# Weight casts to DRAM started one by one on semaphores of attention exponentials, and a scheduler with three new costs

## The chip, the cores and the metric

One Trainium2 chip; the program runs on all 8 cores, each with one sequence of the batch. The metric is device time in microseconds (us) of the slowest core. In a slow execution the cores of one die show a lower granted clock and the time is longer. A ratio compares the fast runs of two kernels of the same rounds on the same chip; it is not quite the ratio of the quoted medians. "Before" differs between chips, so experiments are compared by their ratios to it, given with a 95% interval.

## The reference, cut to what matters

One decoder layer: 2048 tokens and 16 learned meta tokens, width 1024. Two causal attentions with 8 heads each work on the same normalised input; their outputs are gated, added and projected; then a gated MLP with a short convolution follows.

```python
def hybrid_mixer(h, w_in, ...):
    proj = h @ w_in
    o_mla  = causal_block_attention(q_mla, k_mla, v_mla, MLA_QK_DIM ** -0.5)      # first attention
    o_fox  = causal_block_attention(fq, fk, fv, FOX_HEAD_DIM ** -0.5, cum)        # second attention
    gates  = sigmoid(gate_logit + b_gate)
    merged = g_mla * (o_mla @ w_branch_mla) + g_fox * (o_fox @ w_branch_fox)      # the merge
    return merged @ w_out                                                        # w_o
def conv_glu_ffn(h, w_up, conv_w, conv_b, w_down):                               # w_u, w_dn
    up = h @ w_up
    gate, val = up[..., :D_FF], up[..., D_FF:]
    return (silu(causal_depthwise_conv(gate, conv_w, conv_b)) * val) @ w_down
```

## The kernel before

The weights of merge (w_c), output projection (w_o) and MLP (w_u, w_dn) come in float32. The kernel has them cast by DMAs that GpSimd issues: w_c and w_u from DRAM to the bfloat16 scratches scr_c and scr_u, which are loaded tile by tile later, w_o and w_dn straight into SBUF. The casts of w_c, w_u and w_o, 68 transfers, are meant to run beside the two attentions.

The program doesn't write instructions in their final order. It records them with their dependencies, and a list scheduler with a clock of its own (cost tables for instructions, one serial bus for transfers) chooses each engine's order. Then the order is replayed, and semaphore waits are derived from data dependencies.

```python
def dma(self, eng, out, in_, prio=None, key=None, after=None):      # recorder
    ...
    self._dep(it, [in_], [out])
    if after is not None:
        it.preds.add(after)          # only the scheduler knows of it
# replay:
    if it.dma is not None:
        S.dma(e, it.key, kw["out"], kw["in_"])       # no wait for "after" comes out of this
```

So "after" was a hint. GpSimd was stopped by the order of its own stream and by the transfer that used the same one of eight keys before (idle up to 21.4 us at a time for a cast to scr_u, core 4). The casts were recorded in groups behind each pair of heads:

```python
def cast(n, after):
    ...
    for _ in range(n):
        if casts:
            K.dma("pool", *casts.pop(0), key="pc", after=after)
...
    done = heads_out(g, omT[:, p, c0:c0 + n], ot)
    cast(1 if s < 6 else 2, done)            # first attention, 20 steps
...
    done = heads_out(g, of[:, p, 0:n], ot)   # second attention
    if g == 0 and p < 4:                     # two w_o casts a step in the first group of rows
        ...
    else:                                    # later, three scr_u casts a step
        cast(3, done)
```

The load queue (SyncE) is in order as well: scr_c and scr_u tiles, rows of x, and stores of merge results (scr_h) go through it one behind the other (core 4: a store goes out at 465.87 us, for 0.33 us, and the scr_c load recorded behind it at 466.28).

The softmax here doesn't subtract the row's maximum and nothing guards it: scores larger than these inputs give would overflow.

Of the kernel before, what the change touches and what calls it, by code (L numbers as in the profile page):

```python
# [26 lines left out]
class Sched:  # L27
# [71 lines left out]

    def _add(self, eng, fn, reads, writes, dma_key=None):  # L100
        dma = dma_key is not None
# [4 lines left out]
        else:  # L106
            lst = self.cstream[eng]
            stream = eng
            op = _Op(eng, stream, len(lst) + 1, fn, False)
        deps = set()  # L110
        if dma and lst:
            deps.add(lst[-1])
# [71 lines left out]

    def dma(self, eng, key, out, in_, **kw):
        return self._add(eng, lambda e: e.dma_start(out=out, in_=in_, **kw), [in_], [out], dma_key=key)  # L186

# [134 lines left out]
class Item:  # L322
    __slots__ = ("idx", "alts", "tiles", "preds", "succ", "left", "ready", "dma", "bytes", "done", "start", "end", "eng", "prio", "key")

class Recorder:
    RES = {"pe": 165.0, "act": 100.0, "dve": 72.0, "pool": 45.0, "sp": 0.0}
    SEM = {"pe": 145.0, "act": 98.0, "dve": 107.0, "pool": 144.0, "sp": 120.0}
    SLACK = 10.0
    RATE = 250.0
    LAND = {"sp": 2000.0, "pool": 2300.0}  # L330
# [42 lines left out]
    def _item(self, alts, prio):  # L373
        it = Item()
        it.idx = len(self.items)
        it.alts = alts
        it.tiles = []
        it.preds = set()
        it.succ = []
        it.dma = None  # L380
        it.bytes = 0
        it.done = False
        it.ready = 0.0
        it.end = 0.0
        it.eng = None
        it.prio = prio
        it.key = None
        self.items.append(it)
        return it
# [53 lines left out]
    def cost(self, eng, name, args, kw):  # L443
        if name == "row pair":
            return max(self.cost(eng, "matmul", (), k) for k in args) + 12.0
        o = args[0] if name == "memset" else kw["out"]
# [18 lines left out]
        b16 = all(self._n(v)[1].dtype == BF16 for v in ins) and ap.dtype == BF16  # L465
        rate = 1.0
        if name == "reciprocal":
            rate = 8.0
        elif name in ("tensor_copy", "tensor_scalar", "memset"):
            rate = (0.5 if (not ps or b16) else 1.0)  # L470
            if b16 and not ps:
                rate = 0.25
        elif name == "tensor_tensor" and b16:
            rate = 0.5
        if name == "bn_stats":
            n = self._n(kw["in_"])[0]
        return n * rate * 1.042 + (125.0 if name == "scalar_tensor_tensor" and n > 8 else 66.0)

# [21 lines left out]
    def any(self, alts, prio=None):  # L500
        e0, name, args, kw = alts[0]
        wr = []
        rd = []
        for q in (args if name == "row pair" else (kw,)):
            wr += [q[k] for k in ("out", "accum_out") if isinstance(q.get(k), (View, bass.AP))]
            rd += [v for k, v in q.items() if k not in ("out", "accum_out") and isinstance(v, (View, bass.AP))]
        if name == "memset":
            wr = [args[0]]
        al = []
        for (e, nm, ar, k) in alts:  # L510
            al.append((e, nm, ar, k, self.cost(e, nm, ar, k)))
        it = self._item(al, {e: self._prio(e, prio) for (e, _, _, _) in alts})
        self._dep(it, rd, wr)
        return it
# [14 lines left out]
    def dma(self, eng, out, in_, prio=None, key=None, after=None):  # L529
# [6 lines left out]
        if after is not None:  # L536
            it.preds.add(after)
        return it

    def order(self):  # L540
# [12 lines left out]
        ev = []  # L553
        keyend = {}
        bus = [0.0]
        out = []
# [81 lines left out]
        while ev:  # L638
# [51 lines left out]
            if it.dma is not None:  # L690
# [9 lines left out]
                finish(it, "sp", st, end)  # L700
            else:
                freet[e] = st + dur
                out.append((it, alt))
# [18 lines left out]
    def replay(self):  # L722
        S = self.S

        def res(v):
            return v.at(v.t.slot) if isinstance(v, View) else v

        for it, (e, name, args, kw, _d) in self.done:
            if name == "row pair":
                for q in args:  # L730
                    S.op(e, "matmul", **{k: res(v) for k, v in q.items()})
                continue
            kw = {k: res(v) for k, v in kw.items()}
            if it.dma is not None:
                S.dma(e, it.key, kw["out"], kw["in_"])
            else:
                S.op(e, name, *[res(a) for a in args], **kw)

# [11 lines left out]
GT = ((0, 1, 2, 3), (4, 5, 6), (7, 8, 9), (10, 11, 12), (13, 14, 15, 16))  # L750
MID = (2, 5, 8, 11, 15)
FG = ((16, 384), (400, 384), (784, 384), (1168, 384), (1552, 512))
O_QLAT, O_KVLAT, O_KROPE, O_FQ, O_FK, O_FV, O_FLOG, O_GATE = 0, 384, 512, 544, 1056, 1568, 2080, 2088
# [10 lines left out]
def build_program():  # L764
# [28 lines left out]
    with contextlib.ExitStack() as es:  # L793
# [310 lines left out]
        ATT = {"pe": 2, "act": 3, "": 2}  # L1104

        def head(g, h, lhs, q, V, scale, bias, ot):
            c0, n = gcols(g)
# [4 lines left out]
            for kt in range(ts[-1] + 1):  # L1112
# [4 lines left out]
                kw = {} if bias is None else {"bias": bias(kt)}  # L1117
                K.op("act", "activation", out=pt[:, a:n], in_=ps[:, a:n], func=AF.Exp, scale=scale, **kw)
                if kt >= ts[0]:
# [52 lines left out]

        casts = [(scr_c[c, :, a:a + 1536], d_c[c, :, a:a + 1536]) for c in range(8) for a in (0, 1536)]
        casts += [(scr_u[j, :, a:a + 1024], d_u[j, :, a:a + 1024]) for j in range(NJ) for a in (0, 1024)]

        def cast(n, after):
            K.base = {"": 1.5}
            for _ in range(n):
                if casts:
                    K.dma("pool", *casts.pop(0), key="pc", after=after)  # L1180

        for s, (p, g) in enumerate([(p, g) for g in range(5) for p in (0, 1)] + [(p, g) for p in (2, 3) for g in range(5)]):
# [7 lines left out]
            for b in range(2):  # L1190
                h = 2 * p + b
                kt_ = KT[(p % 2) * 2 + b]
                head(g, h, lambda kt: kt_[:, kt * 128:kt * 128 + 128], qs[b], Vm, 96.0 ** -0.5, None, ot)
            done = heads_out(g, omT[:, p, c0:c0 + n], ot)
            cast(1 if s < 6 else 2, done)
            if s == 9:
# [20 lines left out]
        for i in range(4):  # L1217
            q_ = at(207488 + i * 1024, 512)
            K.op("pool", "memset", q_[64:128, :] if i < 2 else q_[0:64, :], 0.0, prio=2.5)
        QA = ring("qa", 207488, 512, 2)  # L1220
        QB = ring("qb", 209536, 512, 2)
# [9 lines left out]
        def attn_fox(g):  # L1231
# [8 lines left out]
            for p in range(4):  # L1240
# [10 lines left out]
                for b in range(2):  # L1251
                    h = 2 * p + b
                    head(g, h, lambda kt: Kf[:, p, kt * 128:kt * 128 + 128], qs[b], Vf, 0.125, lambda kt: bi[:, kt * 8 + h:kt * 8 + h + 1], ot)
                done = heads_out(g, of[:, p, 0:n], ot)
                if g == 0 and p < 4:
                    K.base = {"": 2.5}
                    for k in (2 * p, 2 * p + 1):
                        K.dma("pool", wo[:, k, :], d_o[:, k * 1024:k * 1024 + 1024], after=done)
                else:
                    cast(3, done)  # L1260
            return of
# [41 lines left out]
        for g in range(5):  # L1303
# [4 lines left out]
            merge(g, ofs[g])  # L1308
        K.close(OF, WC, SG, MG, H16, XS)

        K.base = {"": 6}
# [131 lines left out]
```

## Time and profile before

| | before |
|---|---|
| median of 6 runs | 1183.71 us (1180.92 to 1188.01) |
| spans of the 8 cores, profiled run | 1170.8 to 1181.1 us |
| TensorE busy, slowest core | 1107.8 us of 1181.1 |
| waits of TensorE with no named releaser, slowest core | 8.0 us |

A core's span is the time from its first to its last instruction. In the lines of the profile PE is TensorE, PEld its weight loads, DVE VectorE, ACT ScalarE, POOL GpSimd and SP SyncE; a q behind a name is the engine's sequencer. "Issue" is time in which an engine waited for nothing that the profile names. "Busy" TensorE does not mean TensorE at its peak: from 155 to 236 us on core 3 the row shows it busy for 79.3 of 81 us, but the matmuls started there are only 73.8 us of work (the measure is explained under "Where the time came from"). They are strung out behind the exponentials, with ScalarE busy for 75.2 us.

The profile follows the work back from the last instruction, at each step to what released it. This is a part of that chain, on core 4, around 466 us (start, length, what; all in us):

```profile
462.71 3.10 DVE SB L183 x4
...
465.87 0.33 SPq L186
...
466.28 15.20 DMA SB<-scr_c
...
481.62 5.08 PE PS L183 x40
```

A store of a merge result had to wait for VectorE (462.71); the scr_c load stood behind it in the load queue; and the load then took 15.2 us, while the median of all such loads is 5.4 us. TensorE waited only 0.6 us for it; it went on with attention, busy for 14.0 of the 16 us from 466 to 482 us, with ScalarE busy for 12.8.

### The profile page before, as it was taken

Reading aid. Unit: us, or ns where it says so; the run is one execution under the profiler, and the core shown is the slowest. Engines: PE = TensorE matmul, PEld = TensorE weight load, DVE = VectorE, ACT = ScalarE, POOL = GpSimd, SP = SyncE. Lnnn points to the kernel's source line nnn. Section 1 sums busy time; section 2 is a strip of 40 time slices with the busy share of each in tenths; the row PEclk is TensorE's granted clock in tenths of the full one; section 3 lists DMA queues with packets and bytes.
Section 4 is the critical chain, followed back from the end, with each engine's and each line's share of the span. In section 5 each row is a group of like instructions: output and inputs, shape, how many; then the busy total and the mean of one; then the engine's idle time right before and its main releaser. Section 6 shows DMA issues by size and latency. Waiting matters only on the chain.

```text
span 1181.1 us, 25481 instructions; the slowest of 8 cores (1170.8 to 1181.1 us)
## 1 busy us (share of the span) xinstructions
PE 1107.8 (94%) x8345; PEld 621.5 (53%) x8345; DVE 777.8 (66%) x1737; ACT 637.8 (54%) x1383; POOL 104.3 (9%) x187
## 2 busy tenths in 40 slices
PE   5688999988999998899999999999999999999996
PEld 2344456655555455556566555555446665444442
DVE  5799874655376377486763879756567776567755
ACT  3476689978998657767599335434004443003310
POOL 4111221110021011000000002100000000000000
PEclk8899999999999999999999999999999999999998
DMA  9522385873299539744433636992233333135401
GB/s 216 152 78 70 50 122 87 108 69 49 97 152 154 152 64 193 200 138 147 156 124 121 229 118 173 241 233 91 93 122 126 107 95 104 72 107 167 137 19 54
DMA packets 44497, 147.18 MB, mean 125 GB/s; under 512 B 5665, under 2 KB 6817, under 8 KB 43857
## 3 DMA queue, kind: packets, MB, share of 16 engines
q1 hardware_dynamic: 30114, 115.31, 29.5%
q0 software_dynamic: 14256, 30.23, 20.3%
q8 instruction: 72, 1.18, 0.4%
q14 instruction: 55, 0.45, 0.1%
HBM read 158.91 MB, written 34.67 MB: 164 GB/s over the span
## 4 chain that ended last, share of the span: by engine, by line
PE 81%; DVE 6%; DMA 5%; issue 5%; ACT 3%; POOL 0%; DVEq 0%; POOLq 0%; ACTq 0%; SPq 0%
PE PS L183 81%; DVE SB L183 6%; ACT SB L183 3%; DMA SB<-scr_u 2%; DMA SB<-w_lat 1%; DMA SB<-scr_c 1%; POOL SB L183 0%; DVEq L241 0%; POOL SB L186 0%; ACTq L241 0%; POOLq L222 0%; SPq L186 0%; ACT L183 0%; POOLq L241 0%; SPq L241 0%
## 5 line engine op out<-in xcount | busy, mean ns | idle before, releaser
L183 PE MATMUL PS<-SB 128*128 128x65 bf16 (+8 forms) x8345 | 1107.8, 291 | 62.0 <-DVE SB L183 29.1
L183 PEld LDWEIGHTS PS<-SB 128*128 128x128 bf16 (+1 forms) x8345 | 621.5, 98 | 547.8 <-issue 145.7
L183 ACT ACTIVATE SB<-PS,SB 128x384 bf16<-128x384 f32 (+10 forms) x617 | 312.4, 619 | 234.5 <-PE PS L183 224.7
L183 ACT ACTIVATE SB<-PS 128x384 bf16<-128x384 f32 (+12 forms) x596 | 251.7, 522 | 86.3 <-PE PS L183 83.6
L183 DVE SCALAR_TENSOR_TENSOR SB<-SB 128x1024 f32<-128x1024 f32 (+4 forms) x195 | 183.6, 946 | 21.5 <-POOL SB L183 14.4
L183 ACT ACTIVATE SB<-SB 128x384 f32<-128x384 f32 (+3 forms) x133 | 82.3, 620 | 170.5 <-DVE SB L183 170.2
L183 DVE SCALAR_TENSOR_TENSOR SB<-SB,PS 128x512 f32<-128x512 f32 (+2 forms) x146 | 91.1, 625 | 125.2 <-PE PS L183 86.6
L183 DVE SCALAR_TENSOR_TENSOR SB<-PS,SB 128x384 f32<-128x384 f32 (+1 forms) x220 | 140.5, 641 | 29.8 <-ACT SB L183 21.1
L183 DVE TENSOR_TENSOR SB<-PS,SB 128x384 bf16<-128x384 f32 (+10 forms) x253 | 115.6, 462 | 64.3 <-ACT SB L183 53.6
L183 DVE TENSOR_TENSOR SB<-SB 128x128 bf16<-128x128 bf16 (+8 forms) x348 | 86.9, 273 | 54.0 <-ACT SB L183 46.4
L183 POOL TENSOR_TENSOR SB<-SB 128x1 f32<-128x1 f32 (+2 forms) x67 | 42.5, 634 | 806.2 <-DVE SB L183 806.1
L183 DVE BATCH_NORM_STATS2 SB<-SB 128x6 f32<-128x512 f32 (+1 forms) x100 | 68.7, 689 | 10.2 <-DMA SB<-xm 5.2
L183 DVE CAST SB<-PS 64x384 bf16<-64x384 f32 (+5 forms) x70 | 40.2, 584 | 23.8 <-PE PS L183 23.0
L183 DVE COPY SB<-SB 32x384 bf16<-32x384 bf16 (+2 forms) x80 | 21.3, 267 | 22.1 <-PE PS L183 20.7
L183 DVE COPY SB<-PS 128x2 f32<-128x2 f32 (+6 forms) x73 | 24.1, 330 | 15.5 <-PE PS L183 15.2
L186 POOL DMA_DIRECT2D scr_u<-w_u x44 | 22.9, 528 | 115.4 <-DMA scr_u<-w_u 115.4
L183 DVE RECIPROCAL SB<-PS 128x3 f32<-128x3 f32 (+1 forms) x96 | 16.3, 170 | 15.8 <-PE PS L183 14.4
L183 DVE TENSOR_SCALAR SB<-SB 128x1 f32<-128x1 f32 (+5 forms) x88 | 15.6, 193 | 9.6 <-ACT SB L183 5.2
L186 POOL DMA_DIRECT2D SB<-w_dn x22 | 11.8, 546 | 32.8 <-DMA SB<-w_dn 32.8
L186 POOL DMA_DIRECT2D scr_c<-w_c x16 | 8.4, 529 | 45.0 <-DMA scr_c<-w_c 45.0
L183 DVE BATCH_NORM_AGGREGATE SB<-SB 128x2 f32<-128x12 f32 (+1 forms) x50 | 10.2, 204 | 2.6
L183 POOL MEMSET SB<- 128x112 bf16 (+7 forms) x17 | 9.5, 668 | 11.9 <-DVE SB L183 8.4
(17 smaller groups left out, 28.5 us busy)
## 6 DMA issues: line engine op xcount, KB each, us to landing
SB<-scr_u SPq DMA_DIRECT2D x66, 512.0 KB, 3.9
SB<-scr_c SPq DMA_DIRECT2D x40, 768.0 KB, 5.4
SB<-xm SPq DMA_DIRECT2D x32, 512.0 KB, 6.7
scr_u<-w_u POOLq DMA_DIRECT2D x44, 256.0 KB, 12.1
scr_h<-SB SPq DMA_DIRECT2D x16, 512.0 KB, 6.1
SB<-scr_h SPq DMA_DIRECT2D x16, 512.0 KB, 3.6
out<-SB SPq DMA_DIRECT2D x16, 512.0 KB, 2.6
scr_c<-w_c POOLq DMA_DIRECT2D x16, 384.0 KB, 8.2
```

Source lines behind the costliest of these rows:

```text
L183: return self._add(eng, lambda e: getattr(e, name)(*args, **kw), rd, wr)
L186: return self._add(eng, lambda e: e.dma_start(out=out, in_=in_, **kw), [in_], [out], dma_key=key)
```

## The change

The intent: no groups of casts, but one cast per eleven exponentials over the whole of both attentions, each held back by a real semaphore wait; and a scheduler that counts three more costs. The diff, cut to its core (the removed "row pair" branches were not used by any instruction):

```diff
-    def _add(self, eng, fn, reads, writes, dma_key=None):
+    def _add(self, eng, fn, reads, writes, dma_key=None, after=None):
...
         deps = set()
+        if after is not None:
+            deps.add(after)
...
+    SHIFT = 115.0
...
+            if isinstance(kw.get("scalar1"), (View, bass.AP)):
+                fix += 65.0
...
+        if name == "bn_aggr":
+            fix = 150.0
...
+                if e in shape:                        # act and dve
+                    rw = self.rows(alt[1], alt[2], alt[3])
+                    if rw != shape[e]:
+                        st = max(st, freet[e] + self.SHIFT)
+                        shape[e] = rw
...
-                S.dma(e, it.key, kw["out"], kw["in_"])
+                it.op = S.dma(e, it.key, kw["out"], kw["in_"], after=it.after and it.after.op)
...
+PACE, PACE0 = 11, 40
+        count = [-PACE0]
+        def pace(it):
+            count[0] += 1
+            if count[0] > 0 and count[0] % PACE == 0 and casts:
...
+                K.dma("pool", *casts.pop(0), key="pc", after=it)
...
-                K.op("act", "activation", out=pt[:, a:n], in_=ps[:, a:n], func=AF.Exp, scale=scale, **kw)
+                pace(K.op("act", "activation", out=pt[:, a:n], in_=ps[:, a:n], func=AF.Exp, scale=scale, **kw))
...
-            done = heads_out(g, omT[:, p, c0:c0 + n], ot)
-            cast(1 if s < 6 else 2, done)
+            heads_out(g, omT[:, p, c0:c0 + n], ot)
...
+        casts[0:0] = [(wo[:, k, :], d_o[:, k * 1024:k * 1024 + 1024]) for k in range(8)]
```

The 115, 65 and 150 ns are figures of the scheduler. A whole bn_aggr took 204 ns in the mean (50 of them, core 4 before).

More of the change, by code (lines that the diff above doesn't have):

```diff
@@ L183, in op, with dma @@
         return self._add(eng, lambda e: getattr(e, name)(*args, **kw), rd, wr)
-    def dma(self, eng, key, out, in_, **kw):
-        return self._add(eng, lambda e: e.dma_start(out=out, in_=in_, **kw), [in_], [out], dma_key=key)
+    def dma(self, eng, key, out, in_, after=None, **kw):
+        return self._add(eng, lambda e: e.dma_start(out=out, in_=in_, **kw), [in_], [out], dma_key=key, after=after)
     def barrier_all(self, aps_by_eng=None):
@@ L322 @@
 class Item:
-    __slots__ = ("idx", "alts", "tiles", "preds", "succ", "left", "ready", "dma", "bytes", "done", "start", "end", "eng", "prio", "key")
+    __slots__ = ("idx", "alts", "tiles", "preds", "succ", "left", "ready", "dma", "bytes", "done", "start", "end", "eng", "prio", "key", "after", "op")
 class Recorder:
@@ L387, in _item @@
         it.key = None
+        it.after = None
         self.items.append(it)
@@ L443, in cost @@
     def cost(self, eng, name, args, kw):
-        if name == "row pair":
-            return max(self.cost(eng, "matmul", (), k) for k in args) + 12.0
         o = args[0] if name == "memset" else kw["out"]
@@ L466, in cost @@
         rate = 1.0
+        fix = 125.0 if name == "scalar_tensor_tensor" and n > 8 else 66.0
         if name == "reciprocal":
@@ L476, in cost, with rows @@
             n = self._n(kw["in_"])[0]
-        return n * rate * 1.042 + (125.0 if name == "scalar_tensor_tensor" and n > 8 else 66.0)
+        if name == "bn_aggr":
+            fix = 150.0
+        return n * rate * 1.042 + fix
+    def rows(self, name, args, kw):
+        r = []
+        for v in [args[0] if name == "memset" else kw["out"]] + [kw[k] for k in ("in_", "in0", "in1") if isinstance(kw.get(k), (View, bass.AP))]:
+            ap = self._n(v)[1]
+            ps = ap.ap[0][0]
+            r.append(ap.offset // ps if ps > 0 else 0)
+        return tuple(r[:2])
     def op(self, eng, name, *args, prio=None, claim=(), **kw):
@@ L503, in any @@
         rd = []
-        for q in (args if name == "row pair" else (kw,)):
-            wr += [q[k] for k in ("out", "accum_out") if isinstance(q.get(k), (View, bass.AP))]
-            rd += [v for k, v in q.items() if k not in ("out", "accum_out") and isinstance(v, (View, bass.AP))]
+        wr += [kw[k] for k in ("out", "accum_out") if isinstance(kw.get(k), (View, bass.AP))]
+        rd += [v for k, v in kw.items() if k not in ("out", "accum_out") and isinstance(v, (View, bass.AP))]
         if name == "memset":
@@ L537, in dma @@
             it.preds.add(after)
+            it.after = after
         return it
@@ L554, in order @@
         keyend = {}
+        shape = {"act": None, "dve": None}
         bus = [0.0]
@@ L728, in replay @@
         for it, (e, name, args, kw, _d) in self.done:
-            if name == "row pair":
-                for q in args:
-                    S.op(e, "matmul", **{k: res(v) for k, v in q.items()})
-                continue
             kw = {k: res(v) for k, v in kw.items()}
             if it.dma is not None:
-                S.dma(e, it.key, kw["out"], kw["in_"])
+                it.op = S.dma(e, it.key, kw["out"], kw["in_"], after=it.after and it.after.op)
             else:
-                S.op(e, name, *[res(a) for a in args], **kw)
+                it.op = S.op(e, name, *[res(a) for a in args], **kw)
 D = 1024
@@ L1104, in build_program @@
         ATT = {"pe": 2, "act": 3, "": 2}
+        casts = [(scr_c[c, :, a:a + 1536], d_c[c, :, a:a + 1536]) for c in range(8) for a in (0, 1536)]
+        casts += [(scr_u[j, :, a:a + 1024], d_u[j, :, a:a + 1024]) for j in range(NJ) for a in (0, 1024)]
+        count = [-PACE0]
+        def pace(it):
+            count[0] += 1
+            if count[0] > 0 and count[0] % PACE == 0 and casts:
+                b = K.base
+                K.base = {"": 1.5}
+                K.dma("pool", *casts.pop(0), key="pc", after=it)
+                K.base = b
         def head(g, h, lhs, q, V, scale, bias, ot):
@@ L1171, in q_mla @@
             return qs
-        casts = [(scr_c[c, :, a:a + 1536], d_c[c, :, a:a + 1536]) for c in range(8) for a in (0, 1536)]
-        casts += [(scr_u[j, :, a:a + 1024], d_u[j, :, a:a + 1024]) for j in range(NJ) for a in (0, 1024)]
-        def cast(n, after):
-            K.base = {"": 1.5}
-            for _ in range(n):
-                if casts:
-                    K.dma("pool", *casts.pop(0), key="pc", after=after)
         for s, (p, g) in enumerate([(p, g) for g in range(5) for p in (0, 1)] + [(p, g) for p in (2, 3) for g in range(5)]):
@@ L1253, in attn_fox @@
                     head(g, h, lambda kt: Kf[:, p, kt * 128:kt * 128 + 128], qs[b], Vf, 0.125, lambda kt: bi[:, kt * 8 + h:kt * 8 + h + 1], ot)
-                done = heads_out(g, of[:, p, 0:n], ot)
-                if g == 0 and p < 4:
-                    K.base = {"": 2.5}
-                    for k in (2 * p, 2 * p + 1):
-                        K.dma("pool", wo[:, k, :], d_o[:, k * 1024:k * 1024 + 1024], after=done)
-                else:
-                    cast(3, done)
+                heads_out(g, of[:, p, 0:n], ot)
             return of
@@ L1309, in build_program @@
         K.close(OF, WC, SG, MG, H16, XS)
+        assert not casts
         K.base = {"": 6}
```

## The prediction

> **What bounds the kernel now.** I read the slices of the page first, then the busy time by stage, the issue waits and spans of all cores, and at last the timelines of GpSimd and TensorE. The page's slices (29.5 us each, tenths busy) show TensorE full from slice 19 on, and holes only before:
>
> ```profile
> PE   5688999988999998899999999999999999999996
> PEclk8899999999999999999999999999999999999998
> DMA  9522385873299539744433636992233333135401
> ```
>
> The same by stage on the slowest core, core 4 (columns: stretch, its length, busy us and instructions of TensorE, weight loads, VectorE, ScalarE, GpSimd, then clock, DMA share, GB/s):
>
> ```profile
> 0.00:118.00 118.00, 88.05 (x532) 42.32 (x533) 93.89 (x195) 62.70 (x137) 28.05 (x49) 0.93 0.50 129
> 118.00:236.00 118.00, 112.92 (x1232) 70.25 (x1230) 80.27 (x280) 101.24 (x271) 21.59 (x36) 1.00 0.66 91
> 236.00:295.00 59.00, 49.09 (x551) 31.52 (x548) 31.46 (x117) 48.20 (x130) 6.16 (x12) 0.94 0.54 59
> 295.00:413.00 118.00, 110.19 (x1058) 63.73 (x1056) 60.56 (x194) 98.15 (x228) 12.02 (x23) 1.00 0.69 138
> 413.00:531.00 118.00, 111.01 (x925) 63.95 (x925) 79.47 (x160) 80.04 (x160) 10.41 (x19) 1.00 0.64 148
> 531.00:590.00 59.00, 58.81 (x513) 35.97 (x512) 40.11 (x82) 39.21 (x83) 1.69 (x3) 1.00 0.44 152
> ```
>
> Idle TensorE: 118.0 - 88.05 = 30 us in the start (LayerNorm and latents), then 5.1 + 9.9 + 7.8 + 7.0 + 0.2 = 30 us in the two attentions and the first merges, and nothing to win in the MLP after 590 us. So the whole change plays for 30 us, 2.5% of the time, plus what a better start gives. Busy TensorE is close to real work too: in the MLP 139 matmuls of 512 columns fill 29.5 us (212 ns each), and an attention key tile needs one 384-column product and three 65-column ones.
>
> Where do those 30 us come from? Not from waits for the data: TensorE waited for a scr_c load 0.6 us and for a scr_u load 2.1 us. The waits that TensorE had with no named releaser differ between cores, and so do the spans:
>
> ```profile
> core 0: 1174.0 us, clock 0.990
> ...
> core 4: 1181.1 us, clock 0.987
> core 5: 1170.8 us, clock 0.989
> core 6: 1175.2 us, clock 0.991
> core 7: 1178.1 us, clock 0.986
> ```
>
> Core 4 has 8.0 us of such issue time in 4 places and core 7 has 5.7 us in 3; cores 0, 2, 5 have 0.2 to 0.6 us, core 1 1.8, core 3 1.0, core 6 none over the list's threshold. The two cores with stalls are the two longest, and the slowest core is the metric. Core 4's longest stall, in fine stretches:
>
> ```profile
> 258.00:260.00 2.00, 2.00 (x26) 1.39 (x25) 1.46 (x6) 2.00 (x7) 0.00 (x0) 1.00 1.07 125
> 260.00:262.00 2.00, 0.08 (x2) 0.00 (x0) 0.00 (x0) 1.24 (x4) 0.00 (x0) 1.00 0.64 61
> 262.00:264.00 2.00, 0.00 (x0) 0.00 (x0) 0.00 (x0) 0.00 (x0) 0.00 (x0) 0.52 1.01 142
> 264.00:266.00 2.00, 1.90 (x17) 1.25 (x17) 0.00 (x0) 1.03 (x3) 1.28 (x3) 0.50 0.20 36
> 266.00:268.00 2.00, 2.00 (x14) 1.19 (x12) 1.32 (x5) 1.27 (x5) 0.27 (x1) 0.50 0.71 67
> ```
>
> The reader is to see that the DMA share is about 1.0 just before and within the hole, that all engines starve behind TensorE, and that the clock then stands at 0.5 for about 6 us: the hole costs 4 us and some 3 more. In 262 to 265 us the queue view has one instruction packet beside 202 packets of the software queue, which carries only weight casts there. The casts come from GpSimd in groups, each group let go when older casts have landed:
>
> ```profile
> 238.81 1.53 POOL L186 DMA_DIRECT2D scr_u<-w_u  x3 [5.92 <-DMA scr_u<-w_u]
> 249.41 0.52 POOL L186 DMA_DIRECT2D scr_u<-w_u  x1 [9.07 <-DMA scr_u<-w_u]
> 251.42 1.53 POOL L186 DMA_DIRECT2D scr_u<-w_u  x3 [1.49 <-DMA scr_u<-w_u]
> 264.70 1.57 POOL L186 DMA_DIRECT2D scr_u<-w_u  x3 [11.74 <-DMA scr_u<-w_u]
> ```
>
> [...] 72 instruction packets with 1.18 MB, 16 KB each. [...] the trace shows 0.5 after the 4.0 us hole. [...]
>
> **The change, part by part.** (1) In the old kernel the "after" of a cast is only a hint to the scheduler; no semaphore enforces it, so GpSimd runs ahead and is stopped only by its eight cast keys. The new one puts a real wait: cast n goes when attention exponential number 40 + 11n is done. There are 16 scr_c, 8 wo and 44 scr_u casts, 68 in all, the last at exponential 788 of 816. Cost: 68 waits on GpSimd, which is 9% busy. Nothing on the path.
> (2) Density. By a count of the exponentials in the trace, the 408 of the first attention run from about 145 to 327 us, 0.45 us each, so one cast each 4.9 us; the 408 of the second from 327 to 650 us, 0.79 us each, so one cast each 8.7 us. The old kernel had 33 casts from 135 to 277 us (4.3 us each), and the 35 others in bursts between 328 and 380 (23) and 434 and 512 us (12). The software queue moved 30.23 MB in 20.3% of 1181 us, 240 us of all engines. In the first attention 16 casts of 0.393 MB and 17 of 0.262 MB (written bytes) are 10.7 MB, an estimate of 85 us in some 160, 53%: hardly less than now, only smoother. In the second, 27 + 8 casts of 0.262 MB are 9.2 MB, 73 us in 320, 23% on top of the loads: the stretch 330 to 380 us, today at a DMA share of 1.01, and 434 to 484 us, at 0.95, come down to about 0.6.
> (3) What that is worth. On the slowest core, the stalls of 4.0, 1.1, 1.05 and 1.85 us and some 3 us of half clock, 11 us. I take half of it as won where the casts stay dense, and what remains is bounded by the other cores: with no stall at all, core 4 would be like cores 0 to 3 and 6, 1172 to 1175 us. So 5 us of the maximum.
> (4) wo moves from 328 to 333 us to exponentials 414 to 491, the 83rd of the second attention, about 367 us in the old trace. Its first use, the out projection of the first group, comes just before the first store of a result at 432 us. It lands in some 13 us, so 50 us early. The last scr_u cast goes at about 625 us; its reader, column block 21, comes near 770 us. Zero.
> (5) The scheduler now knows 115 ns for a change of first partition on ScalarE and VectorE, 65 ns for a tensor scalar and more for a bn_aggr. No instruction gets cheaper; the order changes. In the first 118 us VectorE is the busiest engine (28.6 of 29.5 us in the third slice) and TensorE waits for it; copies that may go to either engine will go more often to ScalarE. From 118 us on, TensorE's waits for ScalarE and VectorE are 16 us. I take a tenth of the two together (some 25 + 16 us): 3 us, by choice and not by measurement. The removed "row pair" branches are unused.
> Sum: 1183.7 - 5 - 3 = 1176 us.
>
> **Rivals.** (a) The bursts are not what stalls TensorE, since six cores have them with under 2 us of stall: then only the scheduler's part counts, 1179 to 1184 us. For it: cores 0 and 4 issue nearly the same casts. Against: the longer stalls all lie between 160 and 450 us, while casts run, none after. (b) A wait takes the place: GpSimd is in order, and a LayerNorm's pow queued behind a cast now waits for an exponential. That delays statistics of a merge, or the landing of scr_u; TensorE would show DMA or VectorE waits, 1185 to 1195 us. Against: GpSimd already waits up to 21.4 us for cast keys with no harm. (c) The new order is worse by luck, or the casts spread to 625 us slow the scr_c loads of the later merges (5.4 us median today): plus 3 to 8 us. (d) The new costs make a much better order and the start loses 10 us as well: 1160 to 1165 us. For it: 30 us idle in the start; against: VectorE itself is 94 us busy in 118.
>
> **Range and chances.** Half of the possible gain is bounded by the cores without stalls, the other by VectorE's own work; so 2% (under 1160 us) needs nearly all of the 30 us. A loss over 2% needs a new stall of 24 us. Range 1166 to 1187 us; faster 0.05, same 0.92, slower 0.03.
>
> **What would show it.** Right: casts single in GpSimd's timeline, 4 to 5 and then 8 to 9 us apart, last near 620 us; DMA share about 0.6 at 330 to 380 us; issue time of TensorE under 2 us on all cores and spans within 5 us of each other; TensorE idle in 118 to 590 us down from 30 to 20 or so. Wrong: equal issue stalls with single casts (rival a), TensorE waiting for scr_u, scr_c, wo or for a pow (b, c), or an idle start well under 25 us (d).

## The result, and the profile after

The changed kernel took 1157.64 us, median of 10 runs (1156.49 to 1294.12, the longest in the slow state); before, in the same rounds and those quoted above, 1184.24 us, median of 20. The ratio of the fast runs is 0.9779 (0.9762 to 0.9797): 2.2% faster. The prediction had 1176 us and a range of 1166 to 1187 us. It was wrong: the direction was right, the size a third of what came, and it had given "faster", by 2% or more, a chance of 0.05.

The page of the changed kernel, the same three rows of slices:

```profile
PE   6699899988899999999999999999999999999996
PEclk9899999999999999999999999999999999999998
DMA  8422435554765467577676817975233322235401
```

Counted from 0, TensorE's slices stand at 9 from slice 11 on, where before slices 15 and 16 (443 to 502 us) stood at 8. Between slices 6 and 22 the DMA row stays between 4 and 8, where it had peaks of 9 and valleys of 2. The stages, on the changed kernel's slowest core, core 1 (same columns as in the prediction):

```profile
0.00:118.00 118.00, 92.24 (x557) 45.71 (x558) 93.82 (x188) 67.03 (x147) 32.49 (x51) 0.96 0.46 127
118.00:236.00 118.00, 110.82 (x1250) 72.18 (x1248) 79.14 (x281) 101.21 (x272) 16.25 (x28) 1.00 0.48 79
236.00:295.00 59.00, 49.86 (x568) 30.40 (x566) 32.55 (x122) 52.27 (x145) 5.98 (x12) 1.00 0.57 87
295.00:413.00 118.00, 113.76 (x1020) 65.27 (x1020) 69.41 (x197) 87.71 (x201) 9.27 (x18) 1.00 0.56 124
413.00:531.00 118.00, 117.49 (x1101) 73.68 (x1098) 81.87 (x179) 99.33 (x208) 10.23 (x19) 1.00 0.73 173
```

Between 413 and 531 us it does 1101 matmuls in place of 925, and TensorE has 0.5 us of idle time in place of 7. All cores gained, and they lie close together now:

```profile
core 0: 1154.6 us, clock 0.992
core 1: 1155.5 us, clock 0.992
...
core 4: 1153.8 us, clock 0.992
...
core 7: 1153.8 us, clock 0.989
```

Core 4 gained 27.3 us, core 0, which had almost no stall, 19.4. The waits of TensorE with no named releaser on the slowest core (us in total, times, longest), before and after:

```profile
PE PS L183 <- issue: 8.0, 4, 4.0
```

```profile
PE PS L185 <- issue: 1.3, 1, 1.3
```

GpSimd's timeline shows casts that come singly, each let go by ScalarE, now and then two:

```profile
249.94 0.53 POOL L188 DMA_DIRECT2D scr_u<-w_u  x1 [4.39 <-ACT SB L185]
253.24 0.52 POOL L188 DMA_DIRECT2D scr_u<-w_u  x1 [2.78 <-ACT SB L185]
261.26 1.05 POOL L188 DMA_DIRECT2D scr_u<-w_u  x2 [7.51 <-ACT SB L185]
266.94 0.52 POOL L188 DMA_DIRECT2D scr_u<-w_u  x1 [4.62 <-ACT SB L185]
```

The median scr_u cast lands in 6.1 us in place of 12.1. The median scr_c load got no faster (5.4 us before, 6.2 after): the long ones went. Of the 39 scr_c loads with a recorded landing, 8 to 11 on each core took over 10 us before, 1 or 2 after. The chain on core 0 in the stretch where the load of 15.2 us had stood on core 4 is TensorE alone:

```profile
424.61 44.08 PE PS L185 x416
...
470.32 73.54 PE PS L185 x691
```

A second place, which the prediction had not seen, is the begin of the MLP. Before, GpSimd let go eight w_dn loads in a row and a ninth when it could, and a scr_u load that met them took 24.2 us, where the median is 3.9 (the first fence is GpSimd's timeline, the second the chain, both of core 4 before):

```profile
730.41 4.29 POOL L186 DMA_DIRECT2D SB<-w_dn  x8
737.65 0.54 POOL L186 DMA_DIRECT2D SB<-w_dn  x1 [2.96 <-DMA SB<-w_dn]
```

```profile
746.83 24.22 DMA SB<-scr_u
771.05 0.14 issue
771.18 18.83 PE PS L183 x112
```

After, w_dn loads come one or two at a time behind a ScalarE instruction (first fence, core 1), and the chain on core 4 from 680 to 790 us is one piece (second fence):

```profile
714.08 1.06 POOL L188 DMA_DIRECT2D SB<-w_dn  x2 [5.40 <-ACT SB L185]
716.35 0.53 POOL L188 DMA_DIRECT2D SB<-w_dn  x1 [1.20 <-ACT SB L185]
```

```profile
679.98 110.14 PE PS L185 x675
```

**Where the time came from.** Busy time misleads here, so I add up work: every matmul that a core has started by a time, each at (columns / 2.4 + 2.5) ns, four times the columns for float32 (14 matmuls), at least 25 ns. These weights are fitted to the traces: on core 3 the median time from one matmul's start to the next is 29 ns for 65 columns, 162 ns for 384, 216 ns for 512 (854 ns in float32) and 25 ns for 8; from 65 to 512 columns that is 187 ns for 447 columns, 1 ns for 2.4. The lead of the changed kernel over the one before, in us of work, on core 3:

| by | 118 us | 295 | 413 | 440 | 470 | 500 | 531 | 590 | 700 | 750 | 800 | 1100 |
|---|---|---|---|---|---|---|---|---|---|---|---|---|
| lead | 5.3 | 0.5 | 6.2 | 7.1 | 10.7 | 16.3 | 17.1 | 17.3 | 17.5 | 17.2 | 20.2 | 20.1 |

Two cores of every trace lack some 72 matmul records; core 3 has all 8345, and so it is used. A lead won in the start is gone by 295 us. The lasting gain is made from there to 531 us, most of it after 385 us (lead 3.6), where merges fill the second attention, and another 3 us from 750 to 800 us. On top of it comes the slowest core: before it was 7.8 us behind core 3, now 2.3 us.

### The profile page after: what moved, and what is told of

Same layout as the page of the kernel before. It is cut to its first block, busy times and chain, and to the rows that moved or that the text cites. A ratio compares the mean times of both kernels' runs of the same rounds, so it can differ in the third digit from the quotient of the medians.

```text
span 1155.5 us, 25513 instructions; the slowest of 8 cores (1151.7 to 1155.5 us)
## 1 busy us (share of the span) xinstructions
PE 1096.1 (95%) x8345; PEld 621.7 (54%) x8345; DVE 772.2 (67%) x1724; ACT 640.6 (55%) x1396; POOL 106.6 (9%) x187
## 3 DMA queue, kind: packets, MB, share of 16 engines
q8 instruction: 72, 1.18, 0.4%
## 4 chain that ended last, share of the span: by engine, by line
PE 89%; issue 3%; DVE 3%; ACT 3%; POOL 1%; DMA 0%; DVEq 0%; POOLq 0%; ACTq 0%
PE PS L185 89%; DVE SB L185 3%; ACT SB L185 3%; POOL SB L185 1%; DMA SB<-lnp 0%; DVEq L243 0%; ACTq L243 0%; POOLq L224 0%; ACT L185 0%; POOLq L243 0%
## 5 line engine op out<-in xcount | busy, mean ns | idle before, releaser
L185 PE MATMUL PS<-SB 128*128 128x65 bf16 (+7 forms) x8345 | 1096.1, 291 | 48.1 <-DVE SB L185 20.6
L185 ACT ACTIVATE SB<-PS,SB 128x384 bf16<-128x384 f32 (+8 forms) x621 | 314.6, 634 | 224.7 <-PE PS L185 210.8
L185 ACT ACTIVATE SB<-PS 128x384 bf16<-128x384 f32 (+12 forms) x605 | 256.2, 535 | 72.2 <-PE PS L185 70.0
L185 DVE TENSOR_TENSOR SB<-PS,SB 128x384 bf16<-128x384 f32 (+8 forms) x253 | 115.6, 462 | 63.2 <-ACT SB L185 51.1
L185 DVE RECIPROCAL SB<-PS 128x3 f32<-128x3 f32 (+2 forms) x96 | 16.6, 173 | 23.7 <-PE PS L185 21.9
L185 DVE COPY SB<-PS 128x2 f32<-128x2 f32 (+6 forms) x66 | 20.4, 311 | 17.0 <-PE PS L185 16.7
L185 DVE TENSOR_SCALAR SB<-SB 128x1 f32<-128x1 f32 (+6 forms) x88 | 15.8, 194 | 7.8 <-ACT SB L185 4.6
```

Source lines behind the costliest of these rows:

```text
L185: return self._add(eng, lambda e: getattr(e, name)(*args, **kw), rd, wr)
```

## The experiments

Eighteen runs were made (no e5 is on record). Three theories stood at first. **W**: the real waits on DMA starts make the gain. **O**: the better costs make a better order. **P** (later **D** and **S**): the spreading of the casts makes it, either because the DMA engines are less crowded (D), or because the scheduler, seeing no groups of casts on its bus, places loads and merges earlier (S).

| run | what | ratio to before (95%) |
|---|---|---|
| changed kernel, first and e15 | | 0.9779 (0.9762 to 0.9797), 0.9768 (0.9739 to 0.9796) |
| e1 | new costs alone | 0.9990 (0.9909 to 1.0071) |
| e2, e16 | changed, old costs | 0.9764 (0.9679 to 0.9850), 0.9805 (0.9775 to 0.9836) |
| e3, e17 | changed order, no waits | 0.9887 (0.9811 to 0.9962), 0.9906 (0.9880 to 0.9932) |
| e4 | old order and groups, all waits | 0.9933 (0.9840 to 1.0026) |
| e6 | old order, single casts with waits | 0.9943 (0.9891 to 0.9994) |
| e7 | changed, waits on casts only | 0.9799 (0.9751 to 0.9846) |
| e19 | changed, waits on other loads only | 0.9880 (0.9855 to 0.9905) |
| e9 | old, waits on w_dn only | 0.9965 (0.9917 to 1.0013) |
| e10 | old, scheduler blind to casts | 0.9971 (0.9945 to 0.9997) |
| e11 | order of e10, single casts, all waits | 0.9841 (0.9817 to 0.9866) |
| e8, e13 | changed, a cast each 6, each 9 exponentials | 0.9973 (0.9930 to 1.0016), 0.9832 (0.9802 to 0.9863) |
| e12 | changed, casts doubled | 1.0395 (1.0334 to 1.0455) |
| e14, e18 | changed, casts in threes | 0.9896 (wrong result), 0.9836 (0.9797 to 0.9875) |

### e1: the new costs alone

Before, with the cost lines and the SHIFT of the diff; nothing else.

> The kernel before, with only the scheduler's new costs (change of first partition, tensor scalar, bn_aggr); casts in groups and all waits as before. Theory W (the real waits on DMA starts make the gain): 1180 to 1186 us, the stalls and the wait of TensorE for scr_u near 770 us stay. Theory O (a better order makes the gain): 1156 to 1165 us. Theory P (the spreading of the casts one by one makes it): 1180 to 1186 us. My guess: 1180 us.

1188.56 us median, ratio 0.9990. The costs by themselves bring nothing that can be seen, and TensorE still stalls, 6.9 us on core 6. Theory O falls as the explanation of the whole gain; the interval leaves room for up to 0.9%.

### e2 and e16: the changed kernel without the new costs

```diff
-                    if rw != shape[e]:
-                        st = max(st, freet[e] + self.SHIFT)
-            if isinstance(kw.get("scalar1"), (View, bass.AP)):
-                fix += 65.0
-        if name == "bn_aggr":
-            fix = 150.0
```

> The changed kernel with the old costs in the scheduler; casts one by one with real waits. Theory W and theory P: 1156 to 1163 us. Theory O: 1178 to 1186 us. My guess: 1162 us.

> The changed kernel with the scheduler's old costs, again, beside the changed one: if the new costs are worth what the TensorE lead at 1100 us says (5 us), 0.980 to 0.983 of before; if nothing, within 0.001 of the changed kernel.

e2 gave 0.9764. Repeated on one chip beside the changed kernel, e16 gave 0.9805 and the changed kernel (e15) 0.9768; the medians of the fast runs are 1161.6 and 1157.5 us. So the costs may be worth some 4 us once the casts are spread, but the intervals overlap, and I don't call that shown. Most of the 2.2% is there without them.

> The changed kernel itself, for comparison on this chip: 0.975 to 0.980 of before.

### e3 and e17: the changed order, without any wait

```diff
-    it.op = S.dma(e, it.key, kw["out"], kw["in_"], after=it.after and it.after.op)
+    it.op = S.dma(e, it.key, kw["out"], kw["in_"], after=None)
```

Every engine has the same instructions in the same order as in the changed kernel; only the waits on "after" are gone.

> The changed kernel with every instruction in the same order on every engine, but the 'after' of a DMA again only a hint: no semaphore wait. Theory W: 1173 to 1180 us, casts run ahead in groups and the w_dn loads bunch up. Theory O: 1156 to 1160 us. Theory P (order of casts alone, without the wait, is enough): 1156 to 1162 us. My guess: 1174 us.

> The changed kernel in its own order without semaphore waits, again, beside the changed one: 0.988 to 0.992 of before, so the waits alone are worth 10 to 14 us in this order.

1176.61 us and 0.9887; 1174.14 us and 0.9906 when repeated. On one chip the waits alone are worth 0.9906 - 0.9768 = 0.0138 of before, 16 us. The rest, 0.9% or 11 us, comes without waits. It isn't purely the order of the compute engines: in GpSimd's own order the casts now stand singly between LayerNorm instructions, which spreads them in part. The stretch from 434 to 484 us on core 3, before, then e17, then the changed kernel:

```profile
434.00:484.00 50.00, 43.29 (x392) 26.02 (x391) 28.94 (x66) 36.31 (x76) 4.94 (x9) 1.00 1.00 207
```

```profile
434.00:484.00 50.00, 48.56 (x412) 29.56 (x411) 32.09 (x72) 34.70 (x74) 2.60 (x5) 1.00 0.73 170
```

```profile
434.00:484.00 50.00, 49.66 (x418) 30.13 (x417) 33.36 (x74) 33.40 (x73) 3.17 (x6) 1.00 0.60 159
```

The DMA share goes from 1.00 over 0.73 to 0.60 and idle TensorE from 6.7 over 1.4 to 0.3 us. What the waits take away shows in the stalls: in e3 seven of eight cores stall for 1.9 to 6.2 us with no releaser, in the changed kernel none for more than 1.3 (up to 4.3 in the repeat e15).

What are these stalls? In e3, core 6 stood for 4.3 us. The queue view of the 0.25 us from 588.00, then TensorE's timeline, then fine stretches:

```profile
q8 instruction: 1, 0.02, 24.9%
```

```profile
585.71 0.74 PE L185 MATMUL PS<-SB 128*128 128x384 bf16 x6
590.75 1.60 PE L185 MATMUL PS<-SB 128*128 128x65 bf16 x6 [4.30 <-issue]
```

```profile
584.00:588.00 4.00, 2.45 (x30) 1.59 (x26) 2.22 (x8) 3.25 (x9) 0.31 (x1) 1.00 1.02 166
588.00:590.00 2.00, 0.00 (x0) 0.00 (x0) 0.01 (x1) 0.00 (x0) 0.20 (x1) 0.85 0.90 225
590.00:592.00 2.00, 1.25 (x6) 0.68 (x7) 0.00 (x0) 0.53 (x1) 0.00 (x0) 0.50 1.09 287
```

A packet of 16 KB of instructions moves at 588.0 us, at a DMA share of 0.9 to 1.0, and TensorE starts 2.5 to 2.75 us later; the clock stands at 0.5 after the hole. Here it fell 2.95 us into the hole; before, on core 4, 2.0 us into that of 4.0 us, and it stayed at 0.5 for 6.8 us, 4.8 of them after the restart. In these 4.8 us the median from the start of a 384-column matmul to the next start is 320 ns (7 of them), in place of 162. By an estimate from these numbers that hole cost 4.0 and another 2.4 us.

Scanning for instruction packets of this queue (q8) around the other long stalls gives the same picture. Before, core 4: packets in the steps that begin at 261.5, 274.0, 354.50 and 445.25 us, restarts at 264.10, 276.73, 356.85 and 447.68. Core 7 before: 219.50 and 242.25, restarts 222.87 and 245.42. The restart follows 2 to 3.4 us behind the packet in every case looked at.

The trace doesn't name the engine that a packet is for, but counting tells. On core 4 before, the trace has 18,438 instructions of TensorE (matmuls, weight loads and those of its sequencer) and 72 packets of this queue, 16 KB each (1.18 MB in all): one for every 256. If the stalls are waits for the next block of TensorE's instructions, they must all end at one place of a count by 256. They do. In the 20 kept traces, on the 120 cores that have every matmul record, TensorE has 156 stalls over 0.8 us with no named releaser. Every one ends at an instruction whose number, divided by 256, leaves 187 to 190, and 2.2 to 3.8 us behind the start of such a packet. So I read these stalls as late refills, waits for the packet with TensorE's next 256 instructions. That denser casts bring more of them is what the doses below show (7.2 to 13.1 us on a core in e8, 10.0 to 29.3 us in e12).

### e4: real waits on the old order

Before, with "after" made a wait for every DMA; casts still in groups of 1 to 3.

> The kernel before in its own order, casts in groups of 1 to 3 after each pair of heads, but every 'after' (casts, w_dn, first loads) is a real semaphore wait. Theory W: 1160 to 1170 us. Theory O: 1180 to 1186 us. Theory P: 1175 to 1182 us, as the casts still come in groups and stop early; only the w_dn part (4 to 5 us) is won. My guess: 1168 us.

1181.19 us, 0.9933 with an interval that reaches 1.0026. TensorE's wait for scr_u near 770 us is gone on all cores, and the stalls are under 1 us on seven cores; on cores 4 and 7 TensorE waits 5.4 and 5.2 us for scr_c. But 13 us short of my guess: groups with waits, on an order made for groups, don't do it. Theory W alone falls.

### e6: single casts on the old order

The replay takes the 68 casts out of GpSimd's stream and puts cast n back behind exponential 40 + 11n with a real wait on it. TensorE, VectorE, ScalarE and the load queue have exactly the order of before.

```diff
+        K.moved = [(it, EX[40 + 11 * (i + 1) - 1]) for i, it in enumerate(MV)]
...
+                S.dma("pool", "pc%d" % (nk[0] % 8), kw["out"], kw["in_"], after=ex.op if ex.idx in gone else None)
```

> The kernel before with its own order on TensorE, VectorE, ScalarE and the load queue, unchanged; only the 68 casts are moved in GpSimd's stream: one by one, each with a real wait on exponential 40 + 11n. All other 'after' stay hints, so the w_dn burst and its 4 to 5 us stay. Theory D (less transfer traffic at a time is the gain): the 413 to 531 us stretch gains 8 to 12 us of TensorE work, total 0.983 to 0.988 of before. Theory S (the scheduler sees other transfer times and makes a better order of the compute engines): 0.995 to 1.00. My guess: 0.987.

0.9943. The long scr_c load has left the chain (1 to 3 of 39 loads now take over 10 us), and the refill stalls are at most 2.3 us, but the stretch from 413 to 531 us gains only 4 us of work on core 3 and nothing on core 1. The guess of 0.987 failed: an order that was made for loads arriving late keeps TensorE as it was, even where they arrive early.

### e10 and e11: an order made as if casts were free

e10 is before with one number changed, so that the scheduler's bus does not see casts from DRAM to DRAM. Nothing is changed in when the chip does them. e11 takes that order and places the casts as e6 does, with waits on the other loads too.

```diff
-        it.bytes = s.nbytes() * (1.0 if eng != "pool" else 1.35 if both else 1.12)
+        it.bytes = s.nbytes() * (1.0 if eng != "pool" else 0.0 if both else 1.12)
```

> The kernel before with one number changed: the scheduler takes the transfer of a cast from DRAM to DRAM as free, so the groups of casts no longer hold up the loads in its own clock; on the chip the casts still come in groups, with no waits. Theory S (the gain in the order came from the scheduler no longer seeing groups of casts in front of the merge's loads): 0.985 to 0.991 of before, like the order of the changed kernel without waits (0.989). Theory 'the order was luck, or an order made in ignorance of real transfers is bad': 0.995 to 1.01.

> The order of e10 (old costs, scheduler blind to the casts) on all compute engines, casts re-placed in GpSimd's stream one by one with a real wait on exponential 40 + 11n, and real waits on the other loads too. If the three parts (order 1.1 per cent, paced casts 0.6 to 0.9, waits on w_dn 0.3) are the whole and add up: 0.976 to 0.981 of before, the changed kernel without any of its new costs. If the scheduler has to see the paced casts: 0.985 or more.

e10: 0.9971, so theory S as I had put it failed. In the scheduler's own clock the new order is 13 us shorter (1117.2 in place of 1130.6 us), but the groups still hit the loads on the chip, and TensorE waits up to 5.5 us for scr_c. e11: 0.9841, thus 1.3% below e10. In the ratios, the sum of e6 (0.6%) and e10 (0.3%), with the w_dn part of e9 (0.35%), is 1.2%, and e11 has 1.6%; the intervals don't let me claim more than a sum. The traces do. This is TensorE's work in two stretches, in us, by the measure used above: mean, lowest and highest of the six cores that have all matmul records, one execution each:

| run | 385 to 531 us | 590 to 800 us |
|---|---|---|
| before | 130.6 (128.6 to 132.0) | 205.7 (204.3 to 206.7) |
| e4, old order, groups, all waits | 128.8 (124.2 to 131.7) | 208.5 (207.9 to 208.8) |
| e6, old order, single casts | 132.3 (131.7 to 133.2) | 203.6 (202.7 to 205.5) |
| e10, blind order, groups | 132.2 (128.6 to 134.8) | 206.0 (203.8 to 207.2) |
| e11, blind order, single casts, all waits | 139.7 (137.2 to 141.4) | 208.8 (208.3 to 209.0) |
| e17, changed order, no waits | 141.0 (139.2 to 142.9) | 202.7 (199.5 to 205.1) |
| e7, changed order, waits on casts | 143.0 (142.9 to 143.2) | 204.2 (201.6 to 206.2) |
| changed kernel | 143.0 (142.9 to 143.1) | 209.1 (208.9 to 209.1) |

In the first stretch single casts alone bring 1.7 us, the blind order alone 1.6, and both 9.1 (e11's waits on the other loads are not what does it: e4 has them too and gains nothing there). So single casts need the order, and the order needs single casts.

In that clock (the length of the scheduler's own plan, known when a kernel is built and not a run on the chip) spreading is worth 12 us with either cost table: 1130.6 to 1118.9 us with the old costs, 1144.5 to 1132.6 us with the new ones. The new costs make its clock 14 us longer; on the chip the time with them is 0.9990 of before (0.9909 to 1.0071, e1).

### e7, e9 and e19: which waits

e7 has waits on the casts alone, e19 on everything but the casts, both in the changed order; e9 adds waits on w_dn alone to the kernel before.

```diff
e7  +  after=it.after.op if it.after and it.dma == "pc" else None
e19 +  after=it.after.op if it.after and it.dma != "pc" else None
```

> The changed kernel, same order, but only the casts have real waits; w_dn and the first loads are let go by hints as before the change. If the w_dn part is worth 4 to 5 us as the work lead after 750 us says: 0.982 of before (the changed kernel had 0.978), TensorE waits 2 to 3 us for scr_u near 770 us. If the waits of the other loads are worth nothing: 0.978.

> The kernel before, same order, with a real wait only on the 22 w_dn loads (each on the Silu activation named by its 'after'). Casts and first loads as before. If TensorE's wait for scr_u near 770 us and the half clock after it come from the burst of w_dn loads: 0.995 to 0.997 of before, the wait gone. If not: 1.000 and the wait stays.

> The changed kernel, same order, real waits on the w_dn and first loads alone, none on the casts. If the parts add up: e3 and e17 (no waits, 0.989 to 0.991) less the w_dn part of 0.003, 0.986 to 0.988 of before, issue stalls of 3 to 6 us as there, no wait for scr_u. If the casts' waits were not needed: 0.977.

e7 0.9799, e9 0.9965, e19 0.9880. In e7 TensorE waits 2.7 to 4.9 us for scr_u on every core; in e9 and e19 at most 1.1 us. (Before, it is 1.9 to 3.1 us. On cores 0, 1 and 7 the clock fell to 0.5 behind 2.5, 2.7 and 2.1 us of that wait and stayed there for 3.41 us; on the others, with waits of 1.9 to 2.7 us, it stayed at 1.00.) Against the changed kernel, the waits on casts are worth 0.9880 - 0.9768 = 1.1% and those on the other loads 0.9799 - 0.9768 = 0.3%, together 1.4%, which is what e17 lost without any. Run by run the 0.3% is inside the interval. The vanished wait, and the table's second stretch, show that it is real: 209.1 us of work in the changed kernel against 204.2 in e7, with no overlap between cores. With the old order it is 208.7 (208.4 to 208.9) in e9 against 205.7 before.

### e8, e12 and e13: the dose

PACE 6 and 9 in place of 11; and, with PACE 11 and the changed order, each of the casts issued a second time behind the same wait, to a scratch that nobody reads.

```diff
-PACE, PACE0 = 11, 40
+PACE, PACE0 = 6, 40
```

```diff
+                if it.dma == "pc":
+                    S.dma(e, "px%d" % (n % 8), self.dummy[n % 8, :, 0:w], kw["in_"], after=it.after.op)
```

(The expectation says that 60 casts are doubled; the 8 w_o casts have the same key and were doubled as well.)

> The changed kernel with a cast every 6 exponentials instead of 11 (one by one, real waits): 61 casts fall in the first attention at a DMA share of about 0.9 there, none after the second attention's start. Theory D: refill stalls and slow loads come back, 0.983 to 0.990 of before. Theory 'one by one is what counts': 0.977 to 0.980.

> The changed kernel, same order on TensorE, VectorE, ScalarE and the load queue, each of the 60 DRAM casts issued a second time, to a scratch that nobody reads, after the same wait. Theory D (late instruction refills and loads come from the density of the casts): 3 to 10 us of issue stalls of TensorE on every core, 0.985 to 0.993 of before. Theory 'the order is all, the chip bears dense casts': 0.978 to 0.981, stalls under 1 us.

> The changed kernel with a cast every 9 exponentials. The scheduler's own clock makes it 4.6 us longer than with 11. Theory S: 0.980 to 0.984 of before. If orders scatter by luck: anywhere from 0.975 to 0.995.

e13 0.9832, e8 0.9973, e12 1.0395: more casts in a given time cost more, far more in e12 than I expected. The clean dose is e12, since in e8 and e13 the order differs too: by the scheduler's own clock e13 is 4.6 us and e8 12 us longer than the changed kernel. e8 packs nearly all casts into the first attention, one by one and each with its wait, at a DMA share of 0.72, 0.96 and 0.89 in 118 to 236, 236 to 295 and 295 to 330 us on core 3. The changed kernel has 0.54, 0.59 and 0.72 there, and no stall over 1.3 us (3.8 us once in its repeat e15). TensorE's stalls on core 2, in e8 and in e12:

```profile
PE PS L185 <- issue: 13.1, 6, 4.2
```

```profile
PE PS L185 <- issue: 29.3, 17, 4.7
...
PE PS L185 <- DMA SB<-w_o: 19.8, 6, 6.6
PE PS L185 <- DMA SB<-scr_c: 11.8, 3, 10.0
```

Over all cores the stalls are 7.2 to 13.1 us in e8 and 10.0 to 29.3 us in e12, whose compute order is that of the changed kernel. Of e8's six listed stalls on core 2, the four longest (214.48, 246.66, 280.67, 330.02 us) again end 2 to 4 us behind an instruction packet (212.0, 243.0, 278.0, 327.5). So density alone makes these stalls; single casts and waits are no protection if there are too many. Not all of e12's loss is stalls: its w_o casts were doubled too, and TensorE waits 12.5 to 24.0 us for w_o and 5.6 to 14.4 us for scr_c.

### e14 and e18: spread, but three at a time

The changed order, the average rate the same; casts are held until the third and let go together on the third one's wait.

> The changed kernel, same order on TensorE, VectorE, ScalarE and the load queue; the casts are let go three at a time, at the place and with the wait of the third of them, so the average rate is the same. If single casts are what keeps the refills of instructions and the loads on time: 0.983 to 0.988 of before, some us of issue stalls. If spreading over the whole attention is enough: 0.977 to 0.980, stalls under 1.5 us.

> As e14, but only the 60 casts to DRAM are let go three at a time (at the place and wait of the third); the 8 wo casts stay single, so the result is right and no wait for wo arises. If single casts keep the refills on time: 0.982 to 0.987 of before and issue stalls of 4 to 8 us as in e14. If spreading alone is enough: 0.976 to 0.979, stalls under 1.5 us.

e14 took two w_o casts along past the point of their first use: its result was wrong, and TensorE waited 6 to 8 us for w_o. Its 0.9896 says nothing on groups. e18 leaves the w_o casts single and is correct: 0.9836, with only 3 of 7 runs fast. Its stalls are 0.0 to 3.4 us, against 0.0 to 4.3 us in e15. It is probably worse than single casts (0.9768 on another chip; the intervals just miss each other), but spreading over the attentions keeps most of the gain. "One by one" is the smaller part of the matter.

## Why the prediction was wrong

- **What bounds the kernel: "So the whole change plays for 30 us".** The sum of idle time was right as a sum and wrong as a limit: core 3 gained 20 us, and its start is still idle for 26 us. Between 434 and 484 us TensorE on core 3 was idle 6.7 us, but the changed kernel did 9.4 us more work there (the lead at 484 us, 15.1, less that at 434 us, 5.7). Time in which TensorE follows ScalarE for want of other work counts as busy (79.3 us for 73.8 us of work from 155 to 236 us).
- **"Not from waits for the data: TensorE waited for a scr_c load 0.6 us".** This is the step that failed most. The wait was short because attention filled it. The chain of waits had the load at 15.2 us in its path, and I had the chain on the page. What the runs show in its place: late loads hardly cost TensorE a wait (at most 2.7 us for scr_c on any core before); they cost it work that could have filled attention. From 385 to 531 us TensorE did 130.6 us of work before and 143.0 after. The late loads are one part of it and the order made around them the other: single casts bring 1.7 us in the old order (e6), and 9.1 us with an order made as if casts were free (e11).
- **(3), worth "5 us of the maximum".** I took the unstalled cores as the floor, 1172 to 1175 us. They came down by 18.8 to 23.5 us themselves, since every core had the late loads and the order made for them. What I had in view there, packets of instructions among those of the casts, fits the count under e3 and the stalls in e8 and e12; but what it does to the slowest core is only part of it. The waits on the casts alone are worth 1.1%, 13 us. One reading was wrong as well: the instruction packet that I counted in 262 to 265 us is one of 8 KB in another queue (q14); the block that ended TensorE's stall (q8, 16 KB) is at 261.8 us.
- **(1), "68 waits on GpSimd ... Nothing on the path".** The cost was right, the reading of the diff was not: the replay passes "after" for every DMA. The waits on w_dn, a further 3 to 4 us, are absent from my sum.
- **(5), 3 us for a better order.** The new costs alone gave nothing (e1), with spread casts perhaps 4 us (e16 against e15). The lead that they make in the start, 5.3 us at 118 us, is gone at 295 us, in the first attention, with ScalarE busy for 101.5 us from 118 to 236 and 52.0 from 236 to 295 us (changed kernel, core 3). What I had not thought of is that the spread casts themselves change the order, by way of the scheduler's bus. Without waits, order and spreading gave 0.9%, 11 us (e17).
- **(2), the density,** was right: the share went from 0.66 to 0.48 in one stage of the first attention and from 0.54 to 0.57 in the other, from 330 to 380 us on core 3 it came down to 0.53 and from 434 to 484 us to the 0.60 forecast.
- **(4), w_o and the last scr_u cast,** was right: w_o goes from 326 to 369 us and nobody waits for it; the last cast goes at 617 us.
- **Rivals.** (a), that the groups aren't what stalls TensorE, is contradicted by e19 against the changed kernel: the order is the same and only the waits on the casts differ, and TensorE stalls for 0.8 to 7.2 us in place of 0.0 to 4.3. (b) and (c) didn't happen. (d) had the size almost right, by luck: it put the gain in the start, where none of it lasts.

In numbers, with the ratios above: waits on casts 1.1%, waits on the other loads 0.3%, order and spreading without waits 0.9%, in all 2.3%. What stays open: how the 0.9% divides between the order of the compute engines and GpSimd's own partial spreading, as no run has the changed order with groups of the old size (e10, whose order is another one, gave 0.9971: that order alone brought little); and whether the new costs do anything.

## What to carry to other kernels

Weight traffic that has no deadline should be held back by real waits on the instruction stream and spread over all the time there is: here the hint in the scheduler didn't hold back an idle GpSimd, and real waits on the casts were worth 1.1%. Don't judge such traffic by the idle time of the busy engine (0.6 us for a load of 15.2 us here); look for long loads in the chain of waits, and count work done by a given time. And give the scheduler the traffic as it will be: the order made for late loads gained 0.6% from single casts (e6), while with the order made as if casts were free they, and the waits on the other loads, brought 1.3% (e11 against e10).
